# Gated linear attention in a two-layer decoder trunk: both heads' queries in one tile, scores on 64 array rows per head, one state product for both heads

## The chip, the cores and the metric

The kernel runs on one core of a Trainium2 chip. The metric is the device time of one execution in microseconds (us); the lower the better.

## What is computed

The program is a two-layer decoder trunk on 1024 tokens of width 1024. Each layer has a mixer (gated linear attention, a short convolution, and latent attention with a causal softmax, gated and projected) and a cross attention into 256 memory tokens. The change concerns the gated linear attention (GLA) alone: four heads with 48 query and key channels and 96 value channels. The reference computes it in chunks:

```python
q_dec = qf * jnp.exp(b)
k_inv = kf * jnp.exp(-b)
k_end = kf * jnp.exp(b_last - b)
A = jnp.where(mask, jnp.einsum('bhncd,bhnjd->bhncj', q_dec, k_inv), 0.0)
o_intra = jnp.einsum('bhncj,bhnjv->bhncv', A, vf)
U = jnp.einsum('bhncd,bhncv->bhndv', k_end, vf)
def step(state, inp):
    u, d = inp
    return d[..., None] * state + u, state
o_inter = jnp.einsum('bhncd,bhndv->bhncv', q_dec, s_prev)
o = o_intra + o_inter
```

`b` is the running sum of the log decays within a chunk, `s_prev` the state before the chunk.

## The kernel before

Activations lie transposed, channels on the 128 partitions and tokens along the free axis, in two halves of 512 tokens (`c`). Nearly every weight product is made in three passes, high by high, high by low and low by high part (`mm3`, lines 313 to 315), on 128x512 operands of type fp32r. The GLA products use plain fp32, and the profile then shows two matmul records and two weight loads for each instruction, except for transposes.

The kernel works on two pairs of heads (`p`), each pair in one tile of 128 channels: head 0 has rows 0 to 63, head 1 rows 64 to 127, 48 channels of each being in use and the rest zero after the scaling by `gqs`. `gla_front` (line 563) computes the decays and scales queries and keys. Since both heads of a pair share one key tile, it makes two query tiles, each with the other head's 64 rows cleared: the vector engine scales `q0` (line 597), the scalar engine copies rows 64 to 127 into `q1` (line 598), and GpSimd clears the two halves (lines 599 and 600). A product over all 128 rows then gives one head's scores.

`gla_body` (line 631) goes through eight steps of 128 tokens (`t`) for a pair. A step consists of the scores `at` (line 650, one matmul for each head, both into one PSUM bank), the causal mask (line 653, a predicated copy into one of two score tiles `atb` that stay zero above the diagonal), the output `o` (line 663: scores by values of each head; line 668: queries by the carried state of each head), the update `up` (line 674), the running state `Q` (line 677 or 679), its decayed copy `st` (line 683) and the eviction `osb` (line 684). There are two pairs, eight steps and two layers: 32 steps, 28 of which have a state to read.

`layers` (line 1259) writes the GLA bodies interleaved with other work: projections of gates (`mg`, `gg`), of values (`gv`) and of the convolution (`cc`, `ch`, `cg`, `cb`). The order in which each engine runs its instructions is then set by the framework's scheduler when the program is built, so that a change of instructions or buffers moves others as well. Each engine runs its own queue in order. PSUM has eight banks: one tagged `mm`, four `S`, two `t`, one `v`; a product whose bank is still to be read waits for the eviction (line 507 for a projection). `BUFS` gives the number of SBUF buffers: 60 tagged `s`, from which the query tiles come.

Of the kernel before, what the change touches and what calls it, by code (L numbers as in the profile page):

```python
# [10 lines left out]
F32 = mybir.dt.float32  # L11
F32R = mybir.dt.float32r
I32 = mybir.dt.int32
U32 = mybir.dt.uint32
AF = mybir.ActivationFunctionType
ALU = mybir.AluOpType
AX = mybir.AxisListType

P = 128
D = 1024  # L20
S = 1024
# [6 lines left out]
DV = 96  # L28
# [34 lines left out]
        pass  # L63


BUFS = {"s": 60, "p": 9, "pt": 4, "tq": 1, "gt": 4}
BANKS = {"mm": 1, "S": 4, "t": 2, "v": 1}


# [15 lines left out]
class Trunk:  # L85
# [14 lines left out]
    def g(self, name, dtype=F32, tag="s", shape=None):  # L100

        return self.sp.tile(shape or [P, 512], dtype, tag=tag, bufs=BUFS[tag], name=name)

# [76 lines left out]
    def setup2(self):  # L180
        nc, A, cp = self.nc, self.A, self.cp
        self.ident = cp.tile([P, P], F32, name="ident")
        nc.sync.dma_start(self.ident, A["c_ident"])
        self.tri = cp.tile([P, P], F32, name="tri")
        nc.sync.dma_start(self.tri, A["c_tri"])
        self.gmask = cp.tile([P, P], F32, name="gmask")
        nc.sync.dma_start(self.gmask, A["c_gmask"])
        cm = self.g("cmaskr", tag="pt", shape=[P, 256])
        nc.sync.dma_start(cm, A["c_cmask"])
        self.cmask = cp.tile([P, 256], mybir.dt.bfloat16, name="cmask")  # L190
        nc.vector.tensor_copy(self.cmask, cm)
        dup = self.g("dupr", tag="pt", shape=[P, P])
        nc.sync.dma_start(dup, A["c_dup"])
        self.dup = cp.tile([P, P], F32R, name="dup")
        nc.vector.tensor_copy(self.dup, dup)
        for l in range(self.depth):
            o = GOFF[(l, "gbias")]
            nc.vector.tensor_scalar(self.ngbias[:, 2 * l : 2 * l + 2], self.gains[:, o : o + 2], -1.0, None, op0=ALU.mult)
        self.atb = []
        for i in range(2):  # L200
            a = cp.tile([P, 2 * P], F32, name=f"atb{i}")
            nc.gpsimd.memset(a, 0.0)
            self.atb.append(a)
        self.atn = 0

    def gain(self, l, what, i=0):
        off = GOFF[(l, what)] + i
        return self.gains[:, off : off + 1]
# [354 lines left out]
    def gla_front(self, l, p):  # L563
        nc = self.nc
        bias = self.gain(l, "gbias", p)

        tot = self.mp.tile([P, 2 * NT], F32, tag="tot", bufs=2, name=f"tot{l}_{p}")
        dec = self.mp.tile([P, NT], F32, tag="dec", bufs=2, name=f"dec{l}_{p}")
        self.dec[p] = dec
        q0 = self.gq[p]  # L570
        q1 = self.g2(f"gq1_{l}_{p}")
        for c in range(2):
            a = self.g(f"gla_a{l}_{p}_{c}", tag="p")
            b = self.g(f"gla_b{l}_{p}_{c}", tag="p")
            ps = self.psum("t", f"z{l}_{p}_{c}")
            nc.tensor.matmul(ps, self.wg[:, p, :], self.glr[c][0:80], start=True, stop=True)
            nc.scalar.activation(a, ps, AF.Abs, bias=bias)
            nc.scalar.activation(b, ps, AF.Relu, bias=self.ngbias[:, 2 * l + p : 2 * l + p + 1], scale=-1.0)
            nc.scalar.activation(a, a, AF.Exp, scale=-1.0)
            nc.scalar.activation(a, a, AF.Ln, bias=1.0)  # L580
            nc.gpsimd.tensor_tensor(b, b, a, op=ALU.add)
            for j in (0, 256):
                js = slice(j, j + 256)
                nc.vector.tensor_tensor_scan(a[:, js], self.cmask, b[:, js], 0.0, op0=ALU.mult, op1=ALU.add)

            tc8 = tot[:, 8 * c : 8 * c + 8]
            nc.vector.tensor_copy(tc8, a.rearrange("p (n c) -> p n c", c=CH)[:, :, CH - 1])
            first = a.rearrange("p (t n c) -> p t n c", n=2, c=CH)[:, :, 0]
            nc.vector.tensor_tensor(
                first, first, tc8.rearrange("p (t n) -> p t n", n=2)[:, :, 0:1].broadcast_to([P, 4, CH]),  # L590
                op=ALU.subtract,
            )
            yield
            nc.scalar.activation(b, a, AF.Exp, scale=-1.0 / TAU)
            nc.scalar.activation(a, a, AF.Exp, scale=1.0 / TAU)

            nc.vector.scalar_tensor_tensor(q0[c], q0[c], self.gain(l, "gqs", p), b, op0=ALU.mult, op1=ALU.mult)
            nc.scalar.copy(q1[c][64:128], q0[c][64:128])
            nc.gpsimd.memset(q1[c][0:64], 0.0)
            nc.gpsimd.memset(q0[c][64:128], 0.0)  # L600
            self.mul(nc.gpsimd, self.gk[p][c], self.gk[p][c], a)
            yield
        n = NT - 1
        ends = tot[:, 1 : 2 * n + 1].rearrange("p (t n) -> p t n", n=2)[:, :, 0]
        starts = tot[:, 2 : 2 * n + 2].rearrange("p (t n) -> p t n", n=2)[:, :, 0]
        nc.vector.tensor_tensor(dec[:, 0:n], ends, starts, op=ALU.add)
        nc.scalar.activation(dec[:, 0:n], dec[:, 0:n], AF.Exp, scale=-1.0 / TAU)
        self.gq[p] = (q0, q1)

    def gla_start(self, l):  # L610

# [19 lines left out]
    def gla_body(self, l, p):  # L631

        nc = self.nc
        q, k, dec = self.gq[p], self.gk[p], self.dec[p]
        Q = None
        st = None
        for t in range(NT):
            c = t // 4
            ts = slice((t % 4) * P, (t % 4 + 1) * P)
# [5 lines left out]
                nc.scalar.copy(kT, ps.rearrange("p (j c) -> p j c", j=4))  # L645
            gv = self.gv[t]
            pair = slice(2 * p * DV, 2 * (p + 1) * DV)
            at = self.psum("S", f"at{l}_{p}_{t}")
            for h in range(2):
                nc.tensor.matmul(at[:, h * P : (h + 1) * P], k[c][:, ts], q[h][c][:, ts], start=True, stop=True)  # L650
            ab = self.atb[self.atn % 2]
            self.atn += 1
            nc.vector.copy_predicated(
                ab.rearrange("p (h c) -> p h c", h=2),
                self.gmask.bitcast(U32).rearrange("p (o c) -> p o c", o=1).broadcast_to([P, 2, P]),
                at[:, : 2 * P].rearrange("p (h c) -> p h c", h=2),
            )
            if t % 2 == 0:
                osb = self.g(f"osb{l}_{p}_{t}", tag="p", shape=[P, 2, 192])
            o = self.psum("v", f"o{l}_{p}_{t}")  # L660
            for h in range(2):
                oc = slice(h * DV, (h + 1) * DV)
                nc.tensor.matmul(
                    o[:, oc], ab[:, h * P : (h + 1) * P], gv[:, (2 * p + h) * DV : (2 * p + h + 1) * DV],
                    start=True, stop=st is None, skip_group_check=True,
                )
                if st is not None:
                    nc.tensor.matmul(
                        o[:, oc], q[h][c][:, ts], st[:, oc], start=False, stop=True, skip_group_check=True,
                    )  # L670
            if t < NT - 1:

                u = self.psum("S", f"up{l}_{p}_{t}")
                nc.tensor.matmul(u[:, 0:192], kT[:, t % 4, :], gv[:, pair], start=True, stop=True)
                if Q is None:
                    Q = self.mp.tile([P, 192], F32, tag="Q", bufs=2, name=f"Q{l}_{p}")
                    nc.vector.tensor_copy(Q, u[:, 0:192])
                else:
                    nc.vector.scalar_tensor_tensor(
                        Q, Q, dec[:, t - 1 : t], u[:, 0:192], op0=ALU.mult, op1=ALU.add  # L680
                    )
                st = self.mp.tile([P, 192], F32, tag="st", bufs=3, name=f"st{l}_{p}_{t}")
                nc.scalar.activation(st, Q, AF.Copy, scale=dec[:, t : t + 1])
            nc.scalar.copy(osb[:, t % 2, :], o[:, 0:192])
            if t % 2 == 1:
                sq = self.g(f"osq{l}_{p}_{t}", tag="p", shape=[P, 2, 192])
# [877 lines left out]
```

## Time and profile before

| | us |
|---|---|
| median of 3 runs | 1402.22 (1402.13 to 1402.89) |
| the profiled execution, its own time | 1403.91 |
| its span, first to last instruction | 1402.1 |
| TensorE (PE) busy | 1372.2 |
| TensorE weight loads (PEld) busy | 1121.3 |
| VectorE (DVE) busy | 759.0 |
| ScalarE (ACT) busy | 689.6 |
| GpSimd (POOL) busy | 543.8 |

The span is the time between the first and the last instruction of the program; the difference to the execution's own time is what lies around it. Busy time counts an engine's instructions, without waits. PE and PEld are one engine: a weight load can run beside the matmul ahead of it. In a timeline, instructions that follow one another with the same line and operands share a row, and a matmul's length is longer than its share of the engine, since matmuls are pipelined: what one costs in a stream is the distance from its start to the start of the next. The first of the two numbers before a shape, such as 128\*64, is the number of array rows and columns that a matmul or load takes up. PEclk, or clock in a table of stretches, is the granted TensorE clock as a share of 2.4 GHz.

### The profile page before, as it was taken

The numbers are of one execution on the slowest core, as the hardware profiler recorded it, in microseconds if no ns is written. First come the engines' busy times: TensorE is split into PE (matmuls) and PEld (weight loads), VectorE is DVE, ScalarE is ACT, GpSimd is POOL, SyncE is SP. The second block draws the span as 40 slices with busy tenths as digits, with TensorE's granted clock in tenths as the row PEclk, the third lists the DMA queues.
The fourth block names the chain that finished last, engine by engine and source line by source line (L and its number), as shares of the span: only waits on it lengthen the run. The fifth ranks groups of instructions, "written<-read, shape, count | busy, mean of one in ns | idle before, by whom it ended". The sixth has DMA issues, their size and how long they took to land.

```text
span 1402.1 us, 19559 instructions
## 1 busy us (share of the span) xinstructions
PE 1372.2 (98%) x7068; PEld 1121.3 (80%) x7068; DVE 759.0 (54%) x1435; ACT 689.6 (49%) x1465; POOL 543.8 (39%) x564
## 2 busy tenths in 40 slices
PE   7998999999999999999999999999999999999998
PEld 5876888888776688888878788888887767888886
DVE  6394434364788554545642633535568884554533
ACT  6365533253777433645532753424467773344443
POOL 0234425115556351343342531441365663414320
PEclk9999999999999999999999999999999999999999
DMA  6221222122212254421622121211222123533403
GB/s 215 90 70 53 91 74 65 47 87 68 67 50 67 83 188 128 128 75 46 201 102 68 53 79 51 93 53 45 94 76 61 46 73 110 193 120 122 162 4 121
DMA packets 59953, 126.93 MB, mean 91 GB/s; under 512 B 7344, under 2 KB 14288, under 8 KB 59856
## 3 DMA queue, kind: packets, MB, share of 16 engines
q1 hardware_dynamic: 59856, 125.67, 27.9%
q8 instruction: 56, 0.92, 0.3%
q14 instruction: 41, 0.34, 0.1%
HBM read 95.76 MB, written 29.36 MB: 89 GB/s over the span
## 4 chain that ended last, share of the span: by engine, by line
PE 85%; DVE 7%; ACT 3%; issue 2%; DMA 2%; POOL 1%; SPq 0%; DVEq 0%; POOLq 0%; ACTq 0%
PE op_ps L313 4%; PE op_ps L314 4%; PE op_ps L315 4%; PE av L953 4%; PE pt L939 3%; PE xqps L313 2%; PE xqps L315 2%; PE xqps L314 2%; PE s L313 2%; PE gg_ps L313 2%; PE gg_ps L315 2%; PE gg_ps L314 2%; PE s L315 1%; PE s L314 1%; PE cc_ps L315 1%
## 5 line engine op out<-in xcount | busy, mean ns | idle before, releaser
L149 POOL TENSOR_TENSOR win_l<-win_r,win_h 128x512 fp32r<-128x512 f32 x70 | 95.1, 1380 | 221.7 <-ACT win_h L127 221.7
L910 POOL TENSOR_SCALAR p<-p,sm 128x128 f32<-128x128 f32 (+3 forms) x144 | 87.4, 616 | 63.7 <-DVE sm L908 42.4
L127 ACT CAST win_h<-win_r 128x1024 fp32r<-128x1024 f32 x47 | 49.2, 1049 | 120.3 <-PE gg_ps L314 36.6
L314 PE MATMUL op_ps<-mix_l,wout_h 128*128 128x512 f32 x256 | 99.9, 390 | 0.0
L315 PE MATMUL op_ps<-mix_h,wout_l 128*128 128x512 f32 x256 | 99.8, 390 | 0.0
L313 PE MATMUL op_ps<-mix_h,wout_h 128*128 128x512 f32 x256 | 99.0, 393 | 0.0
L904 ACT ACTIVATE p<-s,nm 128x128 f32<-128x128 f32 (+3 forms) x144 | 83.1, 580 | 27.2 <-DVE nm L900 13.9
L896 DVE TENSOR_REDUCE nm<-s 128x1 f32<-128x128 f32 (+3 forms) x144 | 78.5, 551 | 3.0 <-PE s L315 1.1
L939 PE MATMUL pt<-ident,p 128*128 128x128 f32 x432 | 70.6, 280 | 1.6 <-POOL p L910 1.6
L939 PEld LDWEIGHTS pt<-ident,p 128*128 128x128 f32 x432 | 49.7, 140 | 27.3 <-issue 14.5
L953 PE MATMUL av<-ph,V 128*64 128x256 f32 x480 | 69.6, 375 | 0.0
L149 POOL TENSOR_TENSOR wout_l<-wout_r,wout_h 128x512 fp32r<-128x512 f32 x32 | 43.4, 1377 | 42.5 <-ACT wout_h L127 34.4
L313 PE MATMUL s<-k_h,q_h 128*128 128x128 f32 (+3 forms) x144 | 55.2, 385 | 1.2 <-ACT p L904 0.6
L313 PEld LDWEIGHTS op_ps<-mix_h,wout_h 128*128 128x128 f32 x256 | 47.8, 188 | 10.5 <-issue 0.8
L315 PEld LDWEIGHTS op_ps<-mix_h,wout_l 128*128 128x128 f32 x256 | 48.1, 188 | 10.0
L314 PEld LDWEIGHTS op_ps<-mix_l,wout_h 128*128 128x128 f32 x256 | 48.1, 188 | 9.7
L947 ACT COPY ph<-pt 128x512 f32<-128x512 f32 (+1 forms) x72 | 39.5, 548 | 23.6 <-PE pt L939 20.5
L313 PE MATMUL xqps<-op_x_h,wq_h 128*128 128x512 f32 x128 | 50.5, 395 | 0.0
L315 PE MATMUL xqps<-op_x_h,wq_l 128*128 128x512 f32 x128 | 50.3, 393 | 0.0
L314 PE MATMUL xqps<-op_x_l,wq_h 128*128 128x512 f32 x128 | 50.1, 391 | 0.0
L314 PE MATMUL s<-k_l,q_h 128*128 128x128 f32 (+3 forms) x144 | 49.9, 346 | 0.0
L315 PE MATMUL s<-k_h,q_l 128*128 128x128 f32 (+3 forms) x144 | 49.1, 348 | 0.0
(521 smaller groups left out, 4222.9 us busy)
## 6 DMA issues: line engine op xcount, KB each, us to landing
win_r<-in_w_in SPq DMA_DIRECT2D x47, 512.0 KB, 3.6
wout_r<-in_w_out SPq DMA_DIRECT2D x16, 512.0 KB, 3.9
x<-in_xt SPq DMA_DIRECT2D x16, 256.0 KB, 5.4
op0r<-in_xt SPq DMA_DIRECT2D x16, 256.0 KB, 3.7
hd<-op0r SPq DMA_DIRECT2D x16, 256.0 KB, 3.1
wq_r<-in_w_mem SPq DMA_DIRECT2D x8, 512.0 KB, 4.0
wk_r<-in_w_mem SPq DMA_DIRECT2D x8, 512.0 KB, 3.6
wvm_r<-in_w_mem SPq DMA_DIRECT2D x8, 512.0 KB, 3.7
```

Source lines behind the costliest of these rows:

```text
L127: ins = self.nc.scalar.copy(hi, raw)
L149: return eng.tensor_tensor(lo, src, hi.bitcast(F32), op=ALU.subtract)
L313: nc.tensor.matmul(ps, a[0], b[0], start=first, stop=False, **k)
L314: nc.tensor.matmul(ps, a[0], b[1], start=False, stop=False, **k)
L315: self.last_mm = nc.tensor.matmul(ps, a[1], b[0], start=False, stop=last, **k).ins
L896: nc.vector.tensor_reduce(nm[:, b : b + 1], ps[:, :w], axis=AX.X, op=ALU.max, negate=True)
L904: nc.scalar.activation(x[:, :w], ps[:, :w], AF.Exp, bias=nm[:, 0:1], accum_out=sm[:, b : b + 1])
L910: nc.gpsimd.tensor_scalar(pr[b][:, :w], pr[b][:, :w], sm[:, 0:1], 1.0, op0=ALU.mult, op1=ALU.mult)
L939: nc.tensor.transpose(ps[:, o : o + P], prob[qi][kt // 4][:, (kt % 4) * P : (kt % 4 + 1) * P], self.ident,)
L947: nc.scalar.copy(pt[:, :w], ps[:, :w])
L953: nc.tensor.matmul(av[own if j == 0 else other, q0:256], self.V[kt][:, 64 * h : 64 * h + 64], pt[:, j * 256 : j * 256 + 256 - q0], start=( ...
```

## The change

The second query tile is given up. `gla_front` scales one tile of queries for both heads, and the scalar copies and the clearing on GpSimd go. The scores of a head are a matmul on that head's 64 rows of the query and key tiles, head 0 on rows 0 to 63 and head 1 on rows 64 to 127 of the array, each into a PSUM bank of its own, and the mask is a predicated copy for each head. The state is kept in two tiles for each pair, `stb`, cleared once at the start; only the diagonal blocks (rows of a head, value columns of that head) are ever written, by two scalar instructions. The product of queries and state is then one matmul of 192 columns for both heads in place of two of 96. One `s` buffer is given up.

```diff
--- before.py
+++ after.py
@@ -63,7 +63,7 @@
         pass
 
 
-BUFS = {"s": 60, "p": 9, "pt": 4, "tq": 1, "gt": 4}
+BUFS = {"s": 59, "p": 9, "pt": 4, "tq": 1, "gt": 4}
 BANKS = {"mm": 1, "S": 4, "t": 2, "v": 1}
 
 
@@ -202,6 +202,10 @@
             nc.gpsimd.memset(a, 0.0)
             self.atb.append(a)
         self.atn = 0
+        self.stb = [[cp.tile([P, 2 * DV], F32, name=f"stb{p}_{i}") for i in range(2)] for p in range(2)]
+        for pair in self.stb:
+            for a in pair:
+                nc.gpsimd.memset(a, 0.0)
 
     def gain(self, l, what, i=0):
         off = GOFF[(l, what)] + i
@@ -567,8 +571,7 @@
         tot = self.mp.tile([P, 2 * NT], F32, tag="tot", bufs=2, name=f"tot{l}_{p}")
         dec = self.mp.tile([P, NT], F32, tag="dec", bufs=2, name=f"dec{l}_{p}")
         self.dec[p] = dec
-        q0 = self.gq[p]
-        q1 = self.g2(f"gq1_{l}_{p}")
+        q = self.gq[p]
         for c in range(2):
             a = self.g(f"gla_a{l}_{p}_{c}", tag="p")
             b = self.g(f"gla_b{l}_{p}_{c}", tag="p")
@@ -593,11 +596,7 @@
             yield
             nc.scalar.activation(b, a, AF.Exp, scale=-1.0 / TAU)
             nc.scalar.activation(a, a, AF.Exp, scale=1.0 / TAU)
-
-            nc.vector.scalar_tensor_tensor(q0[c], q0[c], self.gain(l, "gqs", p), b, op0=ALU.mult, op1=ALU.mult)
-            nc.scalar.copy(q1[c][64:128], q0[c][64:128])
-            nc.gpsimd.memset(q1[c][0:64], 0.0)
-            nc.gpsimd.memset(q0[c][64:128], 0.0)
+            nc.vector.scalar_tensor_tensor(q[c], q[c], self.gain(l, "gqs", p), b, op0=ALU.mult, op1=ALU.mult)
             self.mul(nc.gpsimd, self.gk[p][c], self.gk[p][c], a)
             yield
         n = NT - 1
@@ -605,7 +604,6 @@
         starts = tot[:, 2 : 2 * n + 2].rearrange("p (t n) -> p t n", n=2)[:, :, 0]
         nc.vector.tensor_tensor(dec[:, 0:n], ends, starts, op=ALU.add)
         nc.scalar.activation(dec[:, 0:n], dec[:, 0:n], AF.Exp, scale=-1.0 / TAU)
-        self.gq[p] = (q0, q1)
 
     def gla_start(self, l):
 
@@ -645,16 +643,15 @@
                 nc.scalar.copy(kT, ps.rearrange("p (j c) -> p j c", j=4))
             gv = self.gv[t]
             pair = slice(2 * p * DV, 2 * (p + 1) * DV)
-            at = self.psum("S", f"at{l}_{p}_{t}")
+            ats = []
             for h in range(2):
-                nc.tensor.matmul(at[:, h * P : (h + 1) * P], k[c][:, ts], q[h][c][:, ts], start=True, stop=True)
+                hs = slice(64 * h, 64 * h + 64)
+                ats.append(self.psum("S", f"at{l}_{p}_{t}_{h}"))
+                nc.tensor.matmul(ats[h][:, 0:P], k[c][hs, ts], q[c][hs, ts], start=True, stop=True)
             ab = self.atb[self.atn % 2]
             self.atn += 1
-            nc.vector.copy_predicated(
-                ab.rearrange("p (h c) -> p h c", h=2),
-                self.gmask.bitcast(U32).rearrange("p (o c) -> p o c", o=1).broadcast_to([P, 2, P]),
-                at[:, : 2 * P].rearrange("p (h c) -> p h c", h=2),
-            )
+            for h in range(2):
+                nc.vector.copy_predicated(ab[:, h * P : (h + 1) * P], self.gmask.bitcast(U32), ats[h][:, 0:P])
             if t % 2 == 0:
                 osb = self.g(f"osb{l}_{p}_{t}", tag="p", shape=[P, 2, 192])
             o = self.psum("v", f"o{l}_{p}_{t}")
@@ -662,12 +659,10 @@
                 oc = slice(h * DV, (h + 1) * DV)
                 nc.tensor.matmul(
                     o[:, oc], ab[:, h * P : (h + 1) * P], gv[:, (2 * p + h) * DV : (2 * p + h + 1) * DV],
-                    start=True, stop=st is None, skip_group_check=True,
+                    start=h == 0, stop=st is None, skip_group_check=True,
                 )
-                if st is not None:
-                    nc.tensor.matmul(
-                        o[:, oc], q[h][c][:, ts], st[:, oc], start=False, stop=True, skip_group_check=True,
-                    )
+            if st is not None:
+                nc.tensor.matmul(o[:, 0:192], q[c][:, ts], st, start=False, stop=True, skip_group_check=True)
             if t < NT - 1:
 
                 u = self.psum("S", f"up{l}_{p}_{t}")
@@ -679,8 +674,10 @@
                     nc.vector.scalar_tensor_tensor(
                         Q, Q, dec[:, t - 1 : t], u[:, 0:192], op0=ALU.mult, op1=ALU.add
                     )
-                st = self.mp.tile([P, 192], F32, tag="st", bufs=3, name=f"st{l}_{p}_{t}")
-                nc.scalar.activation(st, Q, AF.Copy, scale=dec[:, t : t + 1])
+                st = self.stb[p][t % 2]
+                for h in range(2):
+                    hs, hd = slice(64 * h, 64 * h + 64), slice(h * DV, (h + 1) * DV)
+                    nc.scalar.activation(st[hs, hd], Q[hs, hd], AF.Copy, scale=dec[hs, t : t + 1])
             nc.scalar.copy(osb[:, t % 2, :], o[:, 0:192])
             if t % 2 == 1:
                 sq = self.g(f"osq{l}_{p}_{t}", tag="p", shape=[P, 2, 192])
```

The built order shows what the scheduler makes of it. Rows are named by the line of their own file: in the changed file line 650 is still `at`, line 660 the product of scores and values, line 665 the product of queries and state, 669 `up`, and 317 to 319 are the three passes of a projection. A name such as `at_1_0_0` means pair 1, step 0, head 0.

TensorE, layer 0, from the transposes of pair 1's keys on, before (`at_1_0` is step 0 of pair 1, `o_0_1` step 1 of pair 0):

```order
L643 MATMUL kTps_1_0_1238<-ident,gk_1_0_619 128x128 x4
L650 MATMUL at_1_0_1245<-gq_1_0_486,gk_1_0_619 128x128
L650 MATMUL at_1_0_1245<-gq_0_1_0_877,gk_1_0_619 128x128
L663 MATMUL o_0_1_1140<-gv_1_1034,atb_190 128x96
L668 MATMUL o_0_1_1140<-st_0_0_1133,gq_0_0_192 128x96
L663 MATMUL o_0_1_1140<-gv_1_1034,atb_190 128x96
L668 MATMUL o_0_1_1140<-st_0_0_1133,gq_0_0_0_735 128x96
L313 MATMUL mg_2_ps_1285<-h_x_h_201,win_24_h 128x512
```

and now, from `up` of pair 0 on:

```order
L669 MATMUL up_0_0_1123<-gv_0_1020,kT_0_0_1111 128x192
L650 MATMUL at_0_1_0_1130<-gq_0_0_200,gk_0_0_202 128x128
L650 MATMUL at_0_1_1_1132<-gq_0_0_200,gk_0_0_202 128x128
L669 MATMUL up_0_1_1140<-gv_1_1026,kT_0_0_1111 128x192
L318 MATMUL mg_1_ps_1156<-h_x_l_239,win_23_h 128x512
L319 MATMUL mg_1_ps_1156<-h_x_h_237,win_23_l 128x512
L641 MATMUL kTps_1_0_1233<-ident,gk_1_0_627 128x128 x4
L650 MATMUL at_1_0_0_1240<-gq_1_0_494,gk_1_0_627 128x128
L660 MATMUL o_0_1_1136<-gv_1_1026,atb_190 128x96
L650 MATMUL at_1_0_1_1242<-gq_1_0_494,gk_1_0_627 128x128
L660 MATMUL o_0_1_1136<-gv_1_1026,atb_190 128x96
L665 MATMUL o_0_1_1136<-stb_0_192,gq_0_0_200 128x192
```

In the changed order the two scores of `at_0_1` stand next to each other, and those of `at_1_0` have a product on all 128 rows between them. Over both layers 22 of the 32 steps have their two scores side by side, and 10 have something between them. The four products `o` have become three.

ScalarE, layer 0, where the rotary tables `te` and `to` are made (two loads of activation tables and four sines), before:

```order
L594 ACTIVATE gla_b_0_0_738<-gla_a_0_0_737 128x512
L251 ACT_TABLE_LOAD
L251 ACTIVATE te<-ang 64x512
L252 ACTIVATE to<-ang 64x512
L251 ACTIVATE te<-ang 64x512
L252 ACTIVATE to<-ang 64x512
L253 ACT_TABLE_LOAD
L595 ACTIVATE gla_a_0_0_737<-gla_a_0_0_737 128x512
L594 ACTIVATE gla_b_0_1_819<-gla_a_0_1_818 128x512
```

and now:

```order
L597 ACTIVATE gla_b_0_0_744<-gla_a_0_0_743 128x512
L598 ACTIVATE gla_a_0_0_743<-gla_a_0_0_743 128x512
L597 ACTIVATE gla_b_0_1_822<-gla_a_0_1_821 128x512
L606 ACTIVATE dec_0_742<-dec_0_742 128x7
L127 CAST win_24_h<-win_24_r 128x1024
L581 ACTIVATE gla_b_1_0_878<-z_1_0_879,ngbias 128x512
L598 ACTIVATE gla_a_0_1_821<-gla_a_0_1_821 128x512
L255 ACT_TABLE_LOAD
L255 ACTIVATE te<-ang 64x512
```

The block stood ahead of the exponentials of `gla_a_0_0` and `gla_b_0_1`; it now stands behind them and behind a weight cast.

VectorE, layer 0, up to the eviction of `mg_1_0`, for which a projection on TensorE waits (bank `mm`), before:

```order
L517 SCALAR_TENSOR_TENSOR mg_0s_959<-mg_0_0_957,mg_0s_959 128x512
L584 SCALAR_TENSOR_TENSOR gla_a_1_1_967<-cmask,gla_b_1_1_968 128x256 x2
L149 TENSOR_TENSOR win_7_l<-win_7_r,win_7_h 128x512 x2
L587 COPY tot_1_875<-gla_a_1_1_967 128x8
L517 SCALAR_TENSOR_TENSOR mg_0s_1007<-mg_0_1_1005,mg_0s_1007 128x512
L589 TENSOR_TENSOR gla_a_1_1_967<-gla_a_1_1_967,tot_1_875 128x4x64
L606 TENSOR_TENSOR dec_1_876<-tot_1_875 128x7
L507 TENSOR_TENSOR mg_1_0_1068<-mg_1_ps_1043,h_acc_198 128x512
L653 COPY_PREDICATED atb_188<-gmask,at_0_0_1121 128x256
```

and now:

```order
L521 SCALAR_TENSOR_TENSOR mg_0s_954<-mg_0_0_952,mg_0s_954 128x512
L511 TENSOR_TENSOR mg_0_1_1000<-mg_0_ps_975,h_acc_207 128x512
L587 SCALAR_TENSOR_TENSOR gla_a_1_1_962<-cmask,gla_b_1_1_963 128x256 x2
L149 TENSOR_TENSOR win_7_l<-win_7_r,win_7_h 128x512 x2
L590 COPY tot_1_875<-gla_a_1_1_962 128x8
L592 TENSOR_TENSOR gla_a_1_1_962<-gla_a_1_1_962,tot_1_875 128x4x64
L605 TENSOR_TENSOR dec_1_876<-tot_1_875 128x7
L521 SCALAR_TENSOR_TENSOR mg_0s_1002<-mg_0_1_1000,mg_0s_1002 128x512
L599 SCALAR_TENSOR_TENSOR gq_1_1_495<-gq_1_1_495,gains,gla_b_1_1_963 128x512
L511 TENSOR_TENSOR mg_1_0_1060<-mg_1_ps_1035,h_acc_206 128x512
```

The same instructions stand ahead of the eviction in both; the queries `gq_1_1` and an eviction of `mg_0_1` have joined them, and the mask of step 0 has left.

## Rows read from the trace of the kernel before

**Rows 1.** the page: busy time of the engines; chain of waits by engine

```profile
PE 1372.2 (98%) x7068; PEld 1121.3 (80%) x7068; DVE 759.0 (54%) x1435; ACT 689.6 (49%) x1465; POOL 543.8 (39%) x564
...
PE 85%; DVE 7%; ACT 3%; issue 2%; DMA 2%; POOL 1%; SPq 0%; DVEq 0%; POOLq 0%; ACTq 0%
```

**Rows 2.** stretches: us, busy of PE, PEld, DVE, ACT, POOL, clock, DMA share, GB/s

```profile
110.00:235.00 125.00, 118.89 (x614) 100.97 (x613) 55.88 (x95) 60.40 (x121) 51.20 (x44) 0.97 0.23 73
...
790.00:930.00 140.00, 137.37 (x722) 117.18 (x721) 58.91 (x104) 67.23 (x136) 59.66 (x52) 1.00 0.21 71
```

**Rows 3.** timeline of TensorE, two steps: start, us, engine, line, operands, shapes

```profile
135.47 0.49 PE L674 MATMUL up<-gv,kT 128*128 128x192 f32 x2
135.80 0.61 PE L650 MATMUL at<-gq,gk 128*128 128x128 f32 x4
136.24 0.49 PE L674 MATMUL up<-gv,kT 128*128 128x192 f32 x2
...
138.15 0.36 PE L663 MATMUL o<-gv,atb 128*128 128x96 f32 x2
...
138.96 0.48 PE L313 MATMUL mg_ps<-h_x_h,win_h 128*128 128x512 f32 x1
139.27 0.40 PE L314 MATMUL mg_ps<-h_x_l,win_h 128*128 128x512 f32 x1
```

**Rows 4.** timeline of TensorE in the attention of layer 0

```profile
422.49 0.50 PE L313 MATMUL s<-k_h,q_h 128*128 128x512 f32 x1
422.83 0.39 PE L314 MATMUL s<-k_l,q_h 128*128 128x512 f32 x1
423.06 0.39 PE L315 MATMUL s<-k_h,q_l 128*128 128x512 f32 x1
...
424.94 1.94 PE L953 MATMUL av<-ph,V 128*64 128x256 f32 x16
426.81 0.66 PE L939 MATMUL pt<-ident,p 128*128 128x128 f32 x4
...
428.86 0.27 PE L315 MATMUL s<-k_h,q_l 128*128 128x128 f32 x1
429.06 0.65 PE L953 MATMUL av<-ph,V 128*64 128x256 f32 x4
429.65 0.55 PE L939 MATMUL pt<-ident,p 128*128 128x128 f32 x3
```

**Rows 5.** timeline of the weight loads there [idle before <-releaser]

```profile
429.06 0.20 PEld L953 LDWEIGHTS av<-ph,V 128*64 128x64 f32 x4
429.64 0.31 PEld L939 LDWEIGHTS pt<-ident,p 128*128 128x128 f32 x3 [0.39 <-issue]
```

**Rows 6.** timeline of both around a product on 80 rows

```profile
83.03 0.39 PE L314 MATMUL gv_ps<-h_x_l,win_h 128*128 128x512 f32 x1
83.03 0.19 PEld L576 LDWEIGHTS z<-glr,wg 80*128 80x128 f32 x1
```

**Rows 7.** groups of instructions, DVE and ACT: busy us, mean ns | idle

```profile
L653 DVE COPY_PREDICATED atb<-gmask,at 128x256 f32<-128x256 uint32 x32 | 14.2, 445 | 37.7 <-PE o L663 21.0 <-PE at L650 16.4
...
L598 ACT COPY gq<-gq 64x512 f32<-64x512 f32 x8 | 4.9, 617 | 0.7 <-DVE gq L597 0.5
```

**Rows 8.** timeline of TensorE around that wait

```profile
118.07 0.80 PE L313 MATMUL mg_ps<-h_x_h,win_h 128*128 128x512 f32 x1 [5.63 <-DVE mg L507]
118.66 0.63 PE L314 MATMUL mg_ps<-h_x_l,win_h 128*128 128x512 f32 x1
...
124.45 0.40 PE L313 MATMUL mg_ps<-h_x_h,win_h 128*128 128x512 f32 x1
```

**Rows 9.** stretch right behind that wait (columns as in rows 2)

```profile
118.00:124.20 6.20, 6.13 (x14) 4.80 (x15) 2.26 (x4) 4.84 (x10) 3.31 (x4) 0.50 0.44 159
```

**Rows 10.** timeline of ScalarE: the table loads of the rotary sines

```profile
95.17 1.28 ACT L251 ACT_TABLE_LOAD   x1
...
100.35 0.63 ACT L595 ACTIVATE gla_a<-gla_a 128x512 f32<-128x512 f32 x1
```

## Prediction

> **What bounds the kernel now.** I read the page first, for the busy times and the chain of waits by engine [rows 1]: TensorE is busy for 98% of the span and holds 85% of the chain that ended last; no other engine is busy for more than 54%. So what the change does to TensorE's own time is what counts, and what it takes from ScalarE and GpSimd counts only where TensorE waits for them. The table of stretches for the two layers' GLA parts says the same of the place itself [rows 2]: TensorE 118.9 of 125 us in layer 0 and 137.4 of 140 in layer 1, VectorE and ScalarE at half of that. Then the timeline of TensorE, for what a GLA product costs in the stream. I take the distance from one start to the next, since the printed lengths overlap. Last come the attention, where this kernel already uses part of the array, and the only long wait in these stretches.
>
> **The prices before.** A step's scores are four records and take 136.24 - 135.80 = 0.44 us, 0.11 each; an update of 192 columns takes 135.80 - 135.47 = 0.33 [rows 3]. The output with a state is eight records. From its first start to the second projection product are 1.12 us, less 0.23 for one product of 512 columns (423.06 - 422.83) 0.89 [rows 3, 4].
>
> **Outputs, a gain.** The scores-by-values half stays, 0.445. The state half becomes one product of 192 columns with 128 stationary ones, the shape of the update, 0.33. So 0.775 in place of 0.89: 0.115 saved in each of 28 steps, 3.2 us. The two cleared state tiles of a pair cost four clears at the very start, on GpSimd, before anything waits for it.
>
> **Scores, a loss.** No product in this trace takes 64 rows of the array; the nearest rows are those that take 64 of its columns, `av` [rows 4, 5]. Here is what going there and back costs. Going in: the last product before, of 128 columns, starts at 428.86 and would let the next start 0.11 later, at 428.97; `av` and its first weight load both start at 429.06. The load did not run ahead beside the product, as loads do elsewhere, and 0.09 us passed empty. Inside: four records last 429.65 - 429.06 = 0.59 and sixteen last 426.81 - 424.94 = 1.87, so one more record costs 1.28/12 = 0.107, although 256 columns of the update's kind would take 0.33 x 256/192 = 0.44 for two, 0.22 each. The two halves of the array run side by side, then. Of the 0.59, 0.43 is four records; 0.16 is left, 0.05 for the first load of 64 columns, uncovered, and about 0.10 for waiting until the array is empty on leaving: the next load starts at 429.64, at the very end of `av`. Leaving again: the first load of the next kind is uncovered too; after 422.49 the second product starts 0.34 later in place of 0.23, 0.11 more [rows 4]. The Trainium skill says the same in words (TensorEngine Tiling, Tiling Modes): a change of tiling mode, not of the tile within one, drains the engine. It gives no price, and the trace agrees.
>
> For the scores I take the price of `av`, with a first load of 128 columns at 0.11: 0.09 + 0.11 in, 0.10 + 0.11 out, 0.41 for a visit. The two heads side by side add two slots of 0.11, so a visit takes 0.63 against 0.44 before: 0.19 lost. In the built order 22 steps have that form: 4.2 us. In the other 10 a product on all 128 rows stands between the two heads, so there are two visits, each with two records in a row: 1.26 against 0.44, 0.82 lost each: 8.2 us. Together 12.4. From below, a visit costs no wait at all and the pair runs side by side: 22 x 0.22 = 4.8 gained. From above, the wait is paid and the heads run one after the other: 4.8 more than I take. I take the middle because `av` shows both halves of it, the empty array and the parallel run.
>
> **Queries and masks, nothing.** Eight scalar copies of 0.617 go [rows 7], and sixteen clears on GpSimd; both engines have more than half of the stretch free [rows 2]. The mask is two instructions for one of 0.445 [rows 7]; each lies between half and the whole of that, so VectorE gets 0 to 14 us more over 32 steps. Its cover is the projections that TensorE runs between a step's scores and its output, and VectorE is free for some 150 us in the two stretches. The split copies of the state are ScalarE work of the same kind, with the saved copies against them. If this cover went, TensorE would show waits for `atb` or `stb` in every step.
>
> **The long wait, kept.** In layer 0 TensorE stands for 5.63 us for an eviction of `mg` on VectorE [rows 8], nearly all of its 6.1 us of idleness there. Behind it the granted clock is 0.50, the 1.2 GHz level, for 6.2 us [rows 9]; the engine had just stood idle. From 112.44 to 124.45 are 12.0 us for 15 products that take 3.4 at full clock: 8.6 us lost. The change reorders this very place. But the orders shown above have the same scans, weight splits and gate steps ahead of that eviction, so I let the wait stand as it is. From below it goes: 8.6 gained. From above, ScalarE's block of sines, 100.35 - 95.17 = 5.2 us [rows 10], now falls into the work that the eviction waits for, against four copies (2.5 us) that leave this stretch: up to 2.7 us longer.
>
> **Sum.** 12.4 - 3.2 + 0 = +9.2 us. The profiled execution took 1403.9, 1.7 above the median of the runs, with a span of 1402.1; it would become 1413.1, and the median of 1402.2 about **1411**. A measurement of this kernel can tell some 0.2% (2.8 us) from no change.
>
> **Rivals.**
> 1. *No wait for an empty array on 64 rows.* Two products on different rows would then cost one, with their loads beside other products. For it: a product on 80 rows of the array has its load start with the product before it, with no break, 83.03 and 83.03 [rows 6], so fewer rows alone stop nothing. Against it: that one is set up on the whole array, and `av`, which is not, stops each time. Gain 4.8 + 3.2: 1394. The Trainium skill has a rule for this side as well (TensorE: Matmul & The Clock Gate, Packing small matmuls): products on different row groups start about 4 ns apart and run together. For `av`'s column halves the trace agrees with the running together, not with a free entry.
> 2. *The array empties, and the heads run one after the other.* For it: each plain fp32 product is two records with loads of their own, and 128 columns may leave no room beside the loads. Against it: `av` is of the same type and does run side by side. +14.0: 1416.
> 3. *The long wait goes.* For it: GpSimd loses its clears, VectorE its place behind them. Against it: the chain of gate steps is unchanged. 9.2 - 8.6: 1403, no change. It decides from the point where the eviction comes before TensorE has run out of other products.
> 4. *The change does not do what it says:* 64-row products behave like the 80-row one, neither emptying the array nor running together. Only the 3.2 of the outputs stay: 1399.
>
> **How the numbers follow.** The forecast 0.55, rival 1 0.17, rival 2 0.13, rival 3 0.10, rival 4 0.05. Slower: 0.55 + 0.13 = 0.68. Same: 0.10. Faster: 0.17 + 0.05 = 0.22. The range takes in all but rival 1: from 1398, just under rival 4, to 1419, rival 2 with the long wait 2.7 us longer. The forecast's own range, with the long wait as bounded from above and a visit cheaper by a quarter (42 x 0.41 x 0.25 = 4.3 us), is 1407 to 1414.
>
> **What would show it.** Right: scores under a form 64\*128, their first load right behind an idle stretch of 0.1 us or so on the load queue, 42 such visits, both heads starting within 0.02 us in 22 of them; 28 state products 0.33 apart from the next; a wait of 4 to 8 us for `mg` or for the values' transposes near 115 us. Wrong: loads of scores that start with the product before them (rival 1 or 4), heads 0.22 apart in a pair (rival 2), or TensorE at 1.00 clock without a wait from 110 to 125 us (rival 3).

## Result and the profile after

The changed kernel takes 1409.86 us (median of 4 runs, 1409.35 to 1410.52), the kernel before 1402.22. The ratio is 1.0053, 95% interval 1.0041 to 1.0064: slower by 7.6 us. Run again (`after_again`) it is 1.0043 (1.0030 to 1.0056), 6.2 us. The prediction was 1411 us, slower.

The profiled execution took 1410.52 us, with a span of 1408.7. The page, busy time of the engines and chain of waits by engine, to be set beside [rows 1]:

```profile
PE 1380.1 (98%) x7012; PEld 1115.9 (79%) x7012; DVE 766.2 (54%) x1467; ACT 695.0 (49%) x1485; POOL 535.7 (38%) x552
...
PE 87%; DVE 6%; ACT 3%; DMA 2%; issue 1%; SPq 0%; POOL 0%; DVEq 0%; POOLq 0%; ACTq 0%
```

TensorE has 56 records fewer (28 state products, two records each) and is busy for 7.9 us more. That is a first sign: fewer records, more time. Its loads are busy for 5.4 us less, but 56 of them are gone as well. The stretches of [rows 2] and, last, of [rows 9] (columns as there):

```profile
110.00:235.00 125.00, 119.77 (x584) 95.99 (x583) 55.57 (x110) 63.32 (x133) 46.34 (x38) 0.97 0.21 70
790.00:930.00 140.00, 138.09 (x675) 111.41 (x674) 60.91 (x121) 70.49 (x147) 50.01 (x42) 0.99 0.20 67
118.00:124.20 6.20, 5.16 (x14) 4.19 (x15) 1.52 (x3) 3.75 (x9) 2.51 (x2) 0.50 0.43 155
```

In 125 us TensorE now gets through 584 records where it got through 614, and in 140 us 675 where it got through 722. These counts show the loss too large: each layer has 28 records fewer to do, and layer 1 begins 2.5 us later (its first decay projection at 771.27 us against 768.74). The clock is the same in layer 0 and 0.99 after 1.00 in layer 1. The place behind the long wait in layer 0 is as it was, at 0.50.

**A visit to the 64-row form.** Timeline of TensorE after, the steps of [rows 3] in their new order (start, us, engine, line, operands, shapes):

```profile
134.59 0.49 PE L669 MATMUL up<-gv,kT 128*128 128x192 f32 x2
135.01 0.49 PE L650 MATMUL at<-gq,gk 64*128 64x128 f32 x4
135.43 0.59 PE L669 MATMUL up<-gv,kT 128*128 128x192 f32 x2
135.73 0.53 PE L318 MATMUL mg_ps<-h_x_l,win_h 128*128 128x512 f32 x1
136.09 0.39 PE L319 MATMUL mg_ps<-h_x_h,win_l 128*128 128x512 f32 x1
...
136.85 0.48 PE L650 MATMUL at<-gq,gk 64*128 64x128 f32 x2
137.27 0.46 PE L660 MATMUL o<-gv,atb 128*128 128x96 f32 x2
137.66 0.48 PE L650 MATMUL at<-gq,gk 64*128 64x128 f32 x2
```

and of the weight loads beside it:

```profile
134.37 0.41 PEld L669 LDWEIGHTS up<-gv,kT 128*128 128x128 f32 x2
135.01 0.30 PEld L650 LDWEIGHTS at<-gq,gk 64*128 64x128 f32 x4 [0.23 <-issue]
135.43 0.30 PEld L669 LDWEIGHTS up<-gv,kT 128*128 128x128 f32 x2
...
136.85 0.29 PEld L650 LDWEIGHTS at<-gq,gk 64*128 64x128 f32 x2 [0.17 <-DVE Q L674]
137.26 0.30 PEld L660 LDWEIGHTS o<-gv,atb 128*128 128x128 f32 x2
```

A load normally starts well ahead of its product: the first one of `up` at 134.37, 0.22 before. The scores' first load starts together with them, at 135.01, after 0.23 us without a load, and so does the first load of the `up` behind them, at 135.43. Both ways the first load does not run ahead of its product. The price, from the first `up` to the second projection product (on leaving, the cost shows in the distances behind the scores, so the window has to reach past them): 136.09 - 134.59 = 1.50 us, less two updates of 0.33 and a projection of 0.23, is 0.61 for the pair of scores; 0.44 before. In the split step, 137.66 - 136.85 = 0.81 is one visit with one head and one product `o` of 0.22, so 0.59 for the visit. The prediction had 0.63 for either. In the single records of the trace, the two heads of a pair start 6 to 7 ns apart. The Trainium skill (TensorEngine Tiling, Tiling Modes) states the drain between modes; the trace agrees, in that no load crosses the change of form beside the product ahead of it, and adds the price.

**The long wait** is there, now for the eviction of the values' transposes on ScalarE, and a little shorter than in [rows 8]. Timeline of TensorE after:

```profile
113.52 0.58 PE L660 MATMUL o<-gv,atb 128*128 128x96 f32 x4
119.04 0.90 PE L558 MATMUL gvt<-ident,vf 128*128 128x128 f32 x3 [4.94 <-ACT gv L562]
119.60 0.78 PE L317 MATMUL mg_ps<-h_x_h,win_h 128*128 128x512 f32 x1
```

ScalarE makes that eviction only at 118.53 us. Its queue had stood behind an exponential that waited for VectorE's `dec`, the end of the scans, weight splits and gate steps. Timeline of ScalarE after:

```profile
116.81 0.63 ACT L597 ACTIVATE gla_b<-gla_a 128x512 f32<-128x512 f32 x1 [2.25 <-DVE dec L605]
```

**Masks and state copies.** Groups of instructions by line and form, VectorE and ScalarE (busy us, mean ns | idle):

```profile
L654 DVE COPY_PREDICATED atb<-gmask,at 128x128 f32<-128x128 uint32 x64 | 17.1, 297 | 23.9 <-PE at L650 20.8 <-PE o L660 2.7
...
L680 ACT ACTIVATE stb<-Q,dec 64x96 f32<-64x96 f32 x56 | 20.9, 372 | 27.2 <-DVE Q L674 14.7 <-DVE Q L672 12.1
```

The masks cost VectorE 17.1 us in place of the 14.2 of [rows 7]. Both engines wait for TensorE or for each other; TensorE shows no wait for `atb` or `stb` anywhere.

### The profile page after: what moved, and what is told of

Read it like the earlier page. It is cut to its first block, busy times and chain, and to the rows that moved or that the text cites. A ratio compares the mean times of both kernels' runs of the same rounds, so it can differ in the third digit from the quotient of the medians.

```text
span 1408.7 us, 19480 instructions
## 1 busy us (share of the span) xinstructions
PE 1380.1 (98%) x7012; PEld 1115.9 (79%) x7012; DVE 766.2 (54%) x1467; ACT 695.0 (49%) x1485; POOL 535.7 (38%) x552
## 4 chain that ended last, share of the span: by engine, by line
PE 87%; DVE 6%; ACT 3%; DMA 2%; issue 1%; SPq 0%; POOL 0%; DVEq 0%; POOLq 0%; ACTq 0%
PE op_ps L317 4%; PE op_ps L319 4%; PE op_ps L318 4%; PE av L950 4%; PE pt L936 3%; PE xqps L317 2%; PE xqps L319 2%; PE xqps L318 2%; PE s L317 2%; PE gg_ps L317 2%; PE gg_ps L319 2%; PE gg_ps L318 2%; PE s L319 1%; PE s L318 1%; PE at L650 1%
```

## Experiments

The theory: the scores on 64 rows are the loss, by the price of a visit; the single state product is a gain that covers part of it. Rivals: the heads in series, the extra bank and mask, ScalarE's split copies, or waits that the new order makes.

The start of the program, up to the first decay projection, ends anywhere from 82.6 to 86.7 us in the profiles, and the two profiles of one kernel differ there by up to 1.7 us, so terms of 2 to 4 us are read from stretches of the trace that do not move: from the first update `up` to the first product of the latent keys (`ckv_ps`, the work right behind the GLA part), 30 of the 32 steps. Two rows give one of them; layer 0 of `after_again`, `scores_128`, `state_again` and `head1_first`, timelines of TensorE, one kernel each:

```profile
133.25 0.32 PE L669 MATMUL up<-gv,kT 128*128 128x192 f32 x1
...
245.38 0.39 PE L317 MATMUL ckv_ps<-h_x_h,win_h 128*128 128x512 f32 x1
```

```profile
136.16 0.32 PE L668 MATMUL up<-gv,kT 128*128 128x192 f32 x1
...
243.07 0.39 PE L317 MATMUL ckv_ps<-h_x_h,win_h 128*128 128x512 f32 x1
```

```profile
134.29 0.32 PE L671 MATMUL up<-gv,kT 128*128 128x192 f32 x1
...
248.47 0.39 PE L317 MATMUL ckv_ps<-h_x_h,win_h 128*128 128x512 f32 x1
```

```profile
133.10 0.32 PE L670 MATMUL up<-gv,kT 128*128 128x192 f32 x1
...
244.17 0.39 PE L317 MATMUL ckv_ps<-h_x_h,win_h 128*128 128x512 f32 x1
```

All of them, worked out in the same way (us):

| kernel | median of runs | ratio to before (95%) | stretch, layer 0 | stretch, layer 1 |
|---|---|---|---|---|
| before | 1402.22 | | 108.88 | 108.62 |
| before_again | 1402.07 | 0.9999 (0.9989 to 1.0008) | 108.86 | 108.63 |
| the change | 1409.86 | 1.0053 (1.0041 to 1.0064) | 112.13 | 112.16 |
| after_again | 1409.05 | 1.0043 (1.0030 to 1.0056) | 112.13 | 112.13 |
| scores_128 | 1397.50 | 0.9965 (0.9952 to 0.9978) | 106.91 | 106.92 |
| same_rows | 1412.33 | 1.0067 (1.0052 to 1.0082) | 114.25 | 114.25 |
| state_twice | 1409.32 | 1.0047 (1.0032 to 1.0062) | 114.15 | 114.19 |
| state_again | 1411.29 | 1.0062 (1.0050 to 1.0075) | 114.18 | 114.15 |
| head1_first | 1406.93 | 1.0030 (1.0018 to 1.0042) | 111.06 | 111.09 |
| grouped | 1393.01 | 0.9933 (0.9917 to 0.9950) | 104.09 | 104.11 |
| grouped_again | 1392.54 | 0.9935 (0.9920 to 0.9950) | 104.12 | 104.09 |
| grouped_128 | 1392.64 | 0.9931 (0.9918 to 0.9945) | 103.97 | 103.97 |

The stretches of one kernel agree within 0.05 us between layers and executions (0.26 between the layers of the kernel before, which has one projection product more in layer 0), which the medians do not. They hold the same work in every kernel but the last three: 550 records, 28 more where the state product is taken twice, and only 528 in the grouped ones.

**scores_128.** The scores on all rows, all else as in the change:

```diff
-                hs = slice(64 * h, 64 * h + 64)
-                nc.tensor.matmul(ats[h][:, 0:P], k[c][hs, ts], q[c][hs, ts], start=True, stop=True)
+                nc.tensor.matmul(ats[h][:, 0:P], k[c][:, ts], q[c][:, ts], start=True, stop=True)
```

> The changed kernel with both scores of a step taken over all 128 rows of the one query tile, in the same built order (each score then holds the sum of both heads, which leaves out the separation of the heads). Theory (each visit to the 64-row form empties the array, 42 visits at 0.41 us, scores in two slots): the form 64*128 is gone, a step's scores cost 0.44 us again, and the time falls by 11 to 12.5 us, from 1409.9 to about 1398, some 3 to 4 us under the kernel before. Rival (the loss comes from the moved order, the two masks or the split state copies): it stays at 1408 to 1411.

Measured: 1397.5, and 5.22 + 5.24 = 10.5 us less than the change in the two stretches, which hold the same records in the same order. The loss lies in the 64-row form. What is left of the change is faster than the kernel before by 3.7 us in the stretches, in spite of the second bank, the second mask and the split copies. Rival 4 of the prediction (64 rows cost nothing of their own, 1399) falls too.

**same_rows.** Both heads on rows 0 to 63, so that they can't run side by side:

```diff
-                hs = slice(64 * h, 64 * h + 64)
+                hs = slice(0, 64)
```

> The changed kernel with both scores of a step on rows 0 to 63, in the same built order (head 1's scores are replaced by head 0's). Theory (the two heads of a pair run side by side because their rows differ): the 22 adjacent pairs take four slots in place of two, 22 x 0.22 = 4.7 us more, about 1414.6; the 20 single visits stay as they are. Rival (the heads run one after the other anyway): no change, 1409.9. Second rival (what costs is the change of row group itself): faster than 1409.

Measured: 1412.3; in the stretches 4.2 us more than the change, where the 20 adjacent pairs in them give 20 x 0.22 = 4.4. The order is again that of the change. Its timeline of TensorE at the same place:

```profile
132.95 0.48 PE L669 MATMUL up<-gv,kT 128*128 128x192 f32 x2
133.37 0.71 PE L650 MATMUL at<-gq,gk 64*128 64x128 f32 x4
134.00 0.59 PE L669 MATMUL up<-gv,kT 128*128 128x192 f32 x2
134.30 0.53 PE L318 MATMUL mg_ps<-h_x_l,win_h 128*128 128x512 f32 x1
134.67 0.39 PE L319 MATMUL mg_ps<-h_x_h,win_l 128*128 128x512 f32 x1
```

The same five rows take 134.67 - 132.95 = 1.72 us against 1.50. So on rows 0 to 63 and 64 to 127 the heads do run side by side, and rival 2 (in series) falls. A price for the change of row group falls too: without that change the kernel is slower. The Trainium skill's rule of products on different row groups that run together (TensorE: Matmul & The Clock Gate, Packing small matmuls) agrees as far as that goes. Rival 1, which took it to mean a free entry, falls by the rows above.

**state_twice and state_again.** The state product once for each head, as before:

```diff
-                nc.tensor.matmul(o[:, 0:192], q[c][:, ts], st, start=False, stop=True, skip_group_check=True)
+                for h in range(2):
+                    oc = slice(h * DV, (h + 1) * DV)
+                    nc.tensor.matmul(o[:, oc], q[c][:, ts], st[:, oc], start=False, stop=True, skip_group_check=True)
```

> The changed kernel with the product of queries and state taken once for each head again, 96 columns each, from the same block-diagonal state. Theory (four records at 0.11 in place of two at 0.165): 28 x 0.115 = 3.2 us slower, 1413.1. Rival (the single product saves nothing, since its weight load or a wait takes the place): 1409.9 within 1 us.

By runs this missed: 1409.3, no slower than the change. The stretches say something else, 2.0 us more in each layer. So it was run again, beside the change on one chip:

> State product once per head again, as in state_twice. By runs that kernel was no slower than the change (1409.3 against 1409.9), by stretch it was 2.0 us slower in each layer (114.15 and 114.19 against 112.13 and 112.16). Theory (the single product saves 0.115 us or more in each of 28 steps, and the noise of the start hid it): 3 to 4 us above after_again in the medians, 114.1 to 114.3 in both stretches. Rival (what the stretch loses is won back elsewhere): within 1 us of after_again.

> The changed kernel once more, in the same call as the next three, for a steadier difference. The time up to the first projections of decays differs by some 2 us from one execution to the next (83 to 87 us in the profiles so far), while the stretch from the first update to the first product of the latent keys (ckv) was 112.13 us in layer 0 and 112.16 in layer 1. Theory: 1408 to 1411 us, 112.1 to 112.2 in both stretches; 5 to 9 above the kernel before.

Measured: 1411.3 against 1409.1, 2.2 us more by the medians and 2.05 + 2.02 = 4.1 us more in the stretches, where TensorE runs without a wait. Not all of the 4.1 need be the product, since the scheduler moves some other records as well. A place that both have, timelines of TensorE, `after_again` and then `state_again`:

```profile
148.56 0.58 PE L660 MATMUL o<-gv,atb 128*128 128x96 f32 x4
...
149.57 0.40 PE L319 MATMUL gg_ps<-h_x_h,win_l 128*128 128x512 f32 x1
```

```profile
149.09 0.58 PE L660 MATMUL o<-gv,atb 128*128 128x96 f32 x4
...
150.22 0.39 PE L319 MATMUL gg_ps<-h_x_h,win_l 128*128 128x512 f32 x1
```

These are 1.01 and 1.13 us, 0.12 for the product, or 3.4 us in 28 steps. Whether the other 0.7 is the product in other places or the order was not separated.

In the two profiles the change loses elsewhere what the kernel with two products does not: 1.5 us to its clock in layer 1 (under "Hardware"), and 1.0 between the two layers' GLA parts (524.44 us from `ckv_ps` to the next `z`, against 523.47). The latter is one wait of TensorE in layer 0's cross attention, for VectorE's `xo0r`, which itself waits for a transfer: 1.30 us at 684.65 in `after_again`, 0.32 at 686.75 in `state_again`. So the medians show only a part. The expected 3 to 4 is met by the stretches alone; the rival of no difference falls, where the two ran side by side.

**head1_first.** Head 1's scores are written first; the products are the same, but the scheduler builds 38 visits in place of 42:

```diff
             for h in range(2):
-                hs = slice(64 * h, 64 * h + 64)
                 ats.append(self.psum("S", f"at{l}_{p}_{t}_{h}"))
+            for h in (1, 0):
+                hs = slice(64 * h, 64 * h + 64)
                 nc.tensor.matmul(ats[h][:, 0:P], k[c][hs, ts], q[c][hs, ts], start=True, stop=True)
```

> The same products, but head 1's scores are written first. In the built order 26 steps then have their two scores side by side and 6 have something between them, so 38 visits to the 64-row form in place of 42. Theory (what costs is the visit, 0.62 us each, whether it holds one head or two): 4 x 0.62 = 2.5 us less than after_again, about 1407.5, taken from the two stretches. Rival (what costs is the product on 64 rows, and there are as many): no difference, within 0.5 us in the two stretches.

Measured: 1406.9, 2.1 us less than `after_again`, and 1.07 + 1.04 = 2.1 in the stretches. It is the visit that is paid, 0.53 us for each one saved, and not the product. That is less than the 0.62 taken; by the rows above, two visits of 0.59 become one of 0.61, which saves 0.57. That medians and stretches agree so well is partly chance: this kernel is spared the 1.5 us of clock too and 0.7 us ahead of layer 0's first update, and loses 1.8 between the layers (526.24 us against 524.44), where the wait for `xo0r` is 2.17 us and the granted clock is 0.50 for 3.4 us behind it.

**grouped.** If the visit is what costs, then the scores of four steps go into one visit, in one bank for each head, with one mask for each head and four steps (the score tiles become four times as wide, and three `s` buffers go for them):

```diff
+            if t % 4 == 0:
+                ats = [self.psum("S", f"at{l}_{p}_{t}_{h}") for h in range(2)]
+                for j in range(4):
+                    js = slice(j * P, (j + 1) * P)
+                    for h in range(2):
+                        hs = slice(64 * h, 64 * h + 64)
+                        nc.tensor.matmul(ats[h][:, js], k[c][hs, js], q[c][hs, js], start=True, stop=True)
```

> The changed kernel with the scores of four steps taken together, one PSUM bank for each head, and one mask instruction of 512 columns for each head; three fewer s buffers and wider score tiles. In the built order there are 13 visits to the 64-row form in place of 42. Theory (the price is that of a visit): 13 x 0.41 + 82 slots x 0.11 = 14.3 us against 42 x 0.41 + 84 x 0.11 = 26.4, so 12 us faster than the change, about 1398, under the kernel before. Rival (the price belongs to each score, not to the visit): 1410 or, with waits for the wider masks, more.

> The version with the scores of four steps together once more, beside the kernel before, to have its gain on a second chip: 1391 to 1394 us, 0.6 to 0.8% below the kernel before.

Measured: 1393.0 and 1392.5, ratio 0.9933 and 0.9935, the fastest version that computes everything: 9 to 10 us faster than the kernel before and 17 than the change. That is 5 more than visits can explain, so one more kernel took the 64 rows out again.

**grouped_128.** As grouped, the scores on all rows (`k[c][:, js], q[c][:, js]`):

> As grouped (scores of four steps written together, into one bank for each head), but with all 128 rows of the one query tile for each head's scores. It leaves out the separation of the heads. Grouped was 1393.0, 4.5 below scores_128 (1397.5); 13 visits at 0.41 are 5.3 us and 41 slots of 0.22 are 9.0, together 14.3, where 64 products on 128 rows at 0.22 are 14.1. Theory (with 13 visits the 64-row form only pays for itself, and the rest of what grouped won comes from writing the scores together: banks, masks and the order): within 1 us of grouped, about 1393, and the stretches 104.1 each, as in grouped. Rival (the two heads running side by side is what grouped won): about 1397.5, as scores_128.

Measured: 1392.6, and the stretches within 0.14 us of grouped. Here is one full visit of eight products in the timeline of TensorE, grouped:

```profile
133.99 0.60 PE L641 MATMUL kTps<-ident,gk 128*128 128x128 f32 x4
134.52 1.16 PE L652 MATMUL at<-gq,gk 64*128 64x128 f32 x16
135.61 0.59 PE L671 MATMUL o<-stb,gq 128*128 128x192 f32 x2
135.91 0.53 PE L317 MATMUL mg_ps<-h_x_h,win_h 128*128 128x512 f32 x1
136.27 0.40 PE L318 MATMUL mg_ps<-h_x_l,win_h 128*128 128x512 f32 x1
```

and grouped_128 at the same place:

```profile
133.00 0.60 PE L641 MATMUL kTps<-ident,gk 128*128 128x128 f32 x4
133.44 1.95 PE L651 MATMUL at<-gq,gk 128*128 128x128 f32 x16
135.23 0.49 PE L670 MATMUL o<-stb,gq 128*128 128x192 f32 x2
135.42 0.53 PE L317 MATMUL mg_ps<-h_x_h,win_h 128*128 128x512 f32 x1
135.79 0.39 PE L318 MATMUL mg_ps<-h_x_l,win_h 128*128 128x512 f32 x1
```

136.27 - 133.99 = 2.28 us against 2.79: a full visit is 0.51 cheaper than eight products on all rows. A visit of 0.41 and four slots of 0.22 gives 1.29 against 1.76, 0.47. But the scheduler builds only three such visits out of 13; the others are cut up or hold one head, and over all 13 the 64 rows only pay for themselves.

What grouped has beyond that, about 5 us against scores_128, is in grouped_128 as well: it comes with the scores written together. The trace shows where most of it goes. With four steps' scores due at once, 16 more records stand ahead of the first update in each layer, where TensorE has waits to fill, and the stretch behind it holds 528 records in place of 550, 2.4 us less work at 0.11 a record (the other 6 follow behind the latent keys' first product). Layer 1 from the first decay projection to the first update, scores_128 and then grouped_128 (columns as in [rows 2]):

```profile
767.85:816.49 48.64, 46.77 (x224) 38.65 (x223) 24.54 (x37) 28.14 (x51) 17.92 (x13) 1.00 0.14 49
```

```profile
760.69:809.39 48.70, 48.40 (x240) 40.38 (x238) 25.51 (x37) 28.25 (x51) 17.96 (x13) 1.00 0.16 49
```

The 16 records take no time there: TensorE is busy for 1.6 us more in the same 48.7 us. The stretch is 2.94 us shorter (103.97 against 106.91). The 0.5 us a layer that are left, with fewer masks and banks and another order, weren't taken apart.

**before_again.** The kernel before once more, for a second profile of it:

> The kernel before once more, for a second profile of it. Against the two profiles of the change, its first profile is 3.3 to 3.5 us shorter from the first update to the latent keys in layer 0 and 3.5 in layer 1, but from the first decay projection to the latent keys only 0.3 to 0.5 shorter in layer 0 against 4.2 in layer 1, because the waits ahead of the first update are longer in it (5.90 us at 112 us against 5.21, and 1.57 at 93 us that the change does not have). Theory (these waits belong to the order in which the kernel before is built): the second profile shows 161 us again in layer 0 and 158 in layer 1. Rival (chance of one execution): 158 to 159 us in both layers.

Measured: from the first decay projection to the latent keys 159.54 us in layer 0 and 158.24 in layer 1, where the first profile had 161.10 and 158.22. Neither the theory nor the rival holds in full. The timeline of TensorE in it:

```profile
94.34 0.39 PE L576 MATMUL z<-glr,wg 80*128 80x512 f32 x1
95.71 0.50 PE L313 MATMUL mg_ps<-h_x_h,win_h 128*128 128x512 f32 x1 [0.97 <-ACT gla_b L578]
...
118.33 0.79 PE L313 MATMUL mg_ps<-h_x_h,win_h 128*128 128x512 f32 x1 [4.82 <-DVE mg L507]
```

The wait behind `z` is there again (its order has it, the change's does not). The 5.63 us of [rows 8] were partly chance: here they are 4.82, against 4.94 after. The long wait is as long in both kernels.

## Why the prediction was right, and where its terms were off

The sum by stretches, between the two second profiles (spans 1401.6 and 1407.2, +5.6): the start -0.5; layer 0 from the first decay projection to the first update 50.67 to 49.30, -1.4; its stretch of updates +3.3; layer 1 up to its first update 49.60 to 50.24, +0.6; its stretch +3.5; everything else +0.1. Medians differ by 6.2 to 7.6.

- **Scores, +12.4 predicted.** Right in kind: the form is paid for on entering and on leaving, and the heads run side by side. The size was 10.5 for 30 of the 32 steps, where the forecast for those (20 pairs at 0.19, 10 split steps at 0.82) is 12.0: a visit costs 0.59 to 0.61 (rows above), by head1_first 0.53, and not 0.63. The price of `av` [rows 4, 5], a form that cuts columns, held for a form that cuts rows, within a tenth by the rows.
- **State product, -3.2 predicted.** Right in kind; the stretches give 4.1, 0.145 a step, in place of 0.115. The distances in a place that did not move give 0.12, close to the forecast; the rest may be the order. The sign looked for, each state product 0.33 from the next start, is not there: behind 22 of them the next start follows after 0.22, and the distance behind that one is longer (0.38 at 149.19 us in `after_again`, against 0.23 in a row of projections).
- **Queries and masks, 0.** Right. The masks grew by 2.9 us on VectorE, and TensorE never waits for them.
- **The long wait kept, 0.** Right, at 4.94 us, with clock 0.50 behind it as in [rows 9], and for the reason given: another engine's eviction ends it, but the same chain on VectorE stands ahead of that one. Rival 3 falls. ScalarE's sines did not lengthen it (ScalarE stood idle for 2.25 us ahead of that exponential), the bound from above wasn't reached.
- **What was not in the sum.** Layer 0 changes by -1.4 ahead of its updates: the wait behind `z` near 95 us, 0.97 of it, goes with the new order; the rest was not traced. Layer 1 changes by +0.6 there: without the fall of its clock the way is 0.9 shorter (48.69 us in state_again against 49.60), 0.7 of which are waits, and the lower clock costs 1.5. The prediction looked for waits from 110 us on only, and in layer 0 most closely.

The errors of the terms (1.5 too much for the scores, 0.9 too little for the state, 0.8 for what was not in the sum) all point to a smaller loss, 6.0 in place of 9.2, so that 1411 came out above the 1409.9 and 1409.1 measured.

## What to carry to other kernels

A change of the part of the array that products use is paid for each visit, not for each product: here 0.6 us for a visit with one product for each half, where the two products on the whole array take 0.44. A single visit gains only when it holds several products of each half without a break, and the built order, not the source, says how many visits there are: count them there before you choose the form. Here no version was faster by the 64 rows: grouped only came out even with grouped_128. Small terms are best read between two landmarks with no wait between them, since a noisy start hides them in the medians. But count the instructions between the landmarks too: in the grouped kernels 22 records left the stretch, 16 of them for a wait ahead of it, where they cost nothing.

## Hardware: what was not expected

The same wait can leave the clock alone or not. In layer 1 TensorE waits 1.7 us for the values' eviction in the change and in state_again. In `after_again`, timeline of TensorE and stretch (columns as in [rows 2]):

```profile
804.96 0.55 PE L558 MATMUL gvt<-ident,vf 128*128 128x128 f32 x3 [1.67 <-ACT gv L562]
...
802.00:814.00 12.00, 10.33 (x52) 8.32 (x51) 3.10 (x6) 5.74 (x12) 3.85 (x3) 0.86 0.25 87
```

and in `state_again`, waits of TensorE in layer 1 (us in total, times, longest) and the same stretch:

```profile
PE gvt L558 <- ACT gv L562: 1.7, 1, 1.7
...
802.00:814.00 12.00, 10.33 (x58) 8.43 (x57) 5.21 (x10) 7.55 (x16) 3.85 (x3) 1.00 0.33 110
```

With the same wait and the same busy time, the granted clock is 0.86 in the one, part of the stretch at the 1.2 GHz level, and 1.00 in the other. The two profiles of the change both show the fall, those of scores_128, state_twice, state_again, same_rows and head1_first do not. From the first decay projection of layer 1 to its first update are 50.24 us in `after_again` and 48.69 in `state_again`: 1.5 us. What decides it stays open.
